# A two-layer encoder trunk: all buffers on one address residue, token sums taken from PSUM, and two projections in turns

## The chip, the cores and the metric

The kernel runs on one core of a Trainium2 chip. The metric is the device time of one execution in microseconds (us); lower is better. The core's engines are named as in the profile: PE (TensorE), DVE (VectorE), ACT (ScalarE), POOL (GpSimd) and SP (SyncE, which issues the DMAs here).

## The reference

1024 tokens of 1024 channels go through two layers in float32.

```python
for layer in range(2):
    hn = rms_norm(h, mix_norm[layer])
    mix = hybrid_mixer(hn, ...) if layer == 0 else conformer_conv(hn, ...)
    h = h + mix
    h = h + swiglu(rms_norm(h, ffn_norm[layer]), wg, wu, wd)   # (silu(h wg) * (h wu)) wd, 2816 wide
# conformer_conv: a = h w_pw1 + b; u = a[:1024] * sigmoid(a[1024:]); causal depthwise conv of
# 31 taps over the tokens; layer norm; silu; w_pw2 + b
```

`hybrid_mixer` is gated linear attention beside stick-breaking attention, then one output projection.

## The kernel before, in words

Every large product is made of three matmuls (`mm3`, L204 to L206): a float32 operand is split into a rounded part `hi` and the rest `lo`, and hi·hi, hi·lo and lo·hi are summed in PSUM. ACT writes `hi` (L89, L92), DVE writes `lo` (L90, L93); in the middle stage POOL writes the `lo` of weights. Most matmuls have 512 columns: 8708 in the program. Each reads a weight-side (stationary) and a moving operand from SBUF.

The tokens are handled in two halves of 512. The program has three stages, each with pools of its own. **Stage 1** (0 to about 880 us) holds the attention layer and `f00`, the first FFN for half 0. **Stage 2** (to about 1840 us) holds the output projection of half 1 (`out_project(1)`), the conv module (`pw1`, conv, layer norm, `pw2`) and the FFNs: `f01` (layer 0, half 1), and `f10`, the first half of layer 1's FFN weights for token half 0. **Stage 3** does the rest of layer 1's FFN by a Strassen-like scheme on pairs: sums of token blocks (`t1` to `t4`) are multiplied with sums of weight blocks (`s1` to `s4`) into PSUM tiles `ps1`, `ps2`, `ps3`.

An FFN makes `pg` and `pu` (PSUM) per chunk of 128 hidden columns, then `a` = silu(`pg`)·`pu`, split again, and `po` sums the down projection; DVE adds `po` to the residual `xr` (L228; L1159 in stage 3), which frees one of two PSUM buffers. A norm (`norm_half`) scales `x` by ACT into `xn`, PE transposes it to PSUM (`pt`, L146), and ACT and DVE split it to `hh` and `hl`.

The steps are written in the order given to `run` (L1008); a scheduler that simulates the engines then sets each engine's order, and pools of one stage reuse the addresses of the stage before, so that a first write waits for the last reader of the bytes. Weights are loaded by SP, one step ahead.

The addresses follow from the order and size of the pools. Before, in the program as built, `x` and `h` tiles start at 0 modulo 256 bytes, while `raw`, split weights `ws` and each stage's tiles (`ft`, `act`, `tt`) start at 128, because the pool `small` ahead of them ends there. Of the 8708 wide matmuls, 6848 have their two operands at different residues, and 1860 have both at 128: those in stage 2 and 3 whose `a`, `ap` or `tt` meets a weight. None has both at 0.

Of the kernel before, what the change touches and what calls it, by code (L numbers as in the profile page):

```python
# [18 lines left out]
P = 128  # L19
# [21 lines left out]
def trunk(ctx, tc, x, mix_norm, ffn_norm, hy_w_in, hy_w_gate2, hy_b_gate, hy_gla_norm,  # L41
# [194 lines left out]
    def ffn_steps(l, h, hT, xt, ps, ft, act, use_silu, group, last=NF, early=None):  # L236
# [10 lines left out]
        def chunk(f, ws):  # L247
# [20 lines left out]
            if use_silu:  # L268
                nc.scalar.activation(s, pr[0], AF.Silu)
            else:  # L270
                sigmoid(s, pr[0])
                nc.vector.tensor_mul(s, s, pr[0])  # L272
            nc.vector.tensor_mul(pr[1], s, pr[1])
            at = act(f"a{nm}")
            split(at[:, 0:TH], at[:, TH:T], pr[1])
# [82 lines left out]
    with ExitStack() as es:  # L358
# [84 lines left out]
        dec = gp.tile([P, 2, 16], F32, name="dec")  # L443
# [397 lines left out]

    with ExitStack() as es:
# [4 lines left out]
        cvp = es.enter_context(tc.tile_pool(name="cv2", bufs=8))  # L847
# [97 lines left out]
        def layer_norm(h, res):  # L945
            xn = {}

            def stats(i):
# [48 lines left out]
        def norm_step(h, gcol, name):  # L997
# [9 lines left out]
        c1 = [interleave(conv_steps(1, cs), conv_steps(1, (q,), (q,))) for cs, q in (((0, 2), 1), ((3, 5, 6, 7), 4))]  # L1007
        run([norm_step(0, mixg[1], "c0"), lambda: add_bias(0)] + p0[:2] + [norm_step(1, ffng[0], "f01")]  # L1008
            + interleave(p0[2:] + f01[:25], c0) + interleave(f01[25:31], ln0) + f01[31:]
            + [norm_step(1, mixg[1], "c1"), lambda: add_bias(1)] + p1[:4] + interleave(pw2(0, s0), c1[0])  # L1010
            + [norm_step(0, ffng[1], "f10")] + interleave(p1[4:] + f10[:9], c1[1])
            + interleave(f10[9:13], ln1) + pw2(1, s1) + [norm_step(1, ffng[1], "f11")]
            + f10[13:])
# [5 lines left out]
    with ExitStack() as es:  # L1019
# [3 lines left out]
        tp3 = es.enter_context(tc.tile_pool(name="t3", bufs=1))  # L1023
# [14 lines left out]
        (hha, hla), (hhb, hlb) = hT["f10"], hT["f11"]  # L1038
        k1, k2 = slice(0, 4), slice(4, 8)
        b11, b21, b12, b22 = [(hi[:, k, :], lo[:, k, :]) for hi, lo in ((hha, hla), (hhb, hlb)) for k in (k1, k2)]  # L1040
        t1, t3, t4 = b11, b12, b21
        tt = tp3.tile([P, NK, TH], F32R, name="tt")
        t2 = tt[:, k1, :], tt[:, k2, :]

        def whole(r, b, k):
            nc.vector.tensor_add(r, r32(b[0][:, k, :]), r32(b[1][:, k, :]))
            return r

        raw_t1 = {}

        def token_sums(k):

            r1 = raw_t1[k] = whole(s_tile(f"t1_{k}"), b11, k)
            r3 = whole(ft(f"t3_{k}"), b12, k)
            nc.vector.tensor_sub(r1, r3, r1)
            r2 = whole(ft(f"t2_{k}"), b22, k)
            nc.vector.tensor_sub(r3, r2, r3)
            nc.vector.tensor_sub(r2, r2, r1)
            for t, r in ((t2, r2), (t3, r3)):
                split(t[0][:, k, :], t[1][:, k, :], r)  # L1060

        def token_sum1(k):

            split(t1[0][:, k, :], t1[1][:, k, :], raw_t1[k])

        def token_sum4(k):

            r = whole(ft(f"t4_{k}"), b21, k)
            nc.vector.tensor_sub(r, r, r32(t2[0][:, k, :]))
            nc.vector.tensor_sub(r, r, r32(t2[1][:, k, :]))  # L1070
            split(t4[0][:, k, :], t4[1][:, k, :], r)

        def product(pm, w, b, first=True, alone=False):
            for k in range(4):
                mm3(pm, w[0][:, k, :], w[1][:, k, :], b[0][:, k, :], b[1][:, k, :], first and k == 0, k == 3,
                    skip_group_check=not alone)

        def pair_weights(w, t, f):
# [11 lines left out]
            nc.vector.tensor_sub(a2[:, k1, :], a1[:, k1, :], a2[:, k1, :])  # L1090
# [72 lines left out]
        steps, late = [lambda k=k, f=f: f(k) for f in (token_sums, token_sum1, token_sum4) for k in range(4)], []  # L1163
# [31 lines left out]
```

## Time and profile before

| | |
|---|---|
| median of 3 runs | 2355.47 us (2352.82 to 2357.84) |
| profiled execution | 2351.72 us, its span 2349.9 us |
| mean granted clock of PE | 0.988 |
| busy PE, DVE, ACT, POOL | 97%, 68%, 41%, 20% of the span |

The profile shows one execution. The span runs from its first to its last instruction. Consecutive matmuls overlap in the records, so the pace is read from start to start, not from a duration. [...]

### The profile page before, as it was taken

The numbers are of one execution on the slowest core, as the hardware profiler recorded it, in microseconds if no ns is written. First come the engines' busy times: TensorE is split into PE (matmuls) and PEld (weight loads), VectorE is DVE, ScalarE is ACT, GpSimd is POOL, SyncE is SP. The second block draws the span as 40 slices with busy tenths as digits, with TensorE's granted clock in tenths as the row PEclk, the third lists the DMA queues.
The fourth block names the chain that finished last, engine by engine and source line by source line (L and its number), as shares of the span: only waits on it lengthen the run. The fifth ranks groups of instructions, "written<-read, shape, count | busy, mean of one in ns | idle before, by whom it ended". The sixth has DMA issues, their size and how long they took to land.

```text
span 2349.9 us, 27994 instructions
## 1 busy us (share of the span) xinstructions
PE 2277.6 (97%) x10602; PEld 1856.5 (79%) x10602; DVE 1595.5 (68%) x2612; ACT 958.5 (41%) x1596; POOL 471.4 (20%) x255
## 2 busy tenths in 40 slices
PE   7999999999999999999999998999999699999999
PEld 6788878788888887888888886878877578888887
DVE  6587664877788645456666652698645877777776
ACT  6465545655565424422222244546444222222221
POOL 0000000000000004444444435949532000000000
PEclk9999999999999999999999998999999799999999
DMA  6254454233243234232232222234322133233222
GB/s 204 94 162 144 165 182 137 75 102 118 88 140 103 67 115 165 72 108 90 95 103 82 97 99 67 78 104 135 130 90 86 47 88 99 63 90 98 64 85 90
DMA packets 219637, 247.98 MB, mean 106 GB/s; under 512 B 9669, under 2 KB 169520, under 8 KB 219502
## 3 DMA queue, kind: packets, MB, share of 16 engines
q1 hardware_dynamic: 219502, 246.19, 33.1%
q8 instruction: 83, 1.36, 0.2%
q14 instruction: 52, 0.43, 0.1%
HBM read 219.42 MB, written 26.74 MB: 105 GB/s over the span
## 4 chain that ended last, share of the span: by engine, by line
PE 91%; DVE 5%; ACT 2%; issue 1%; DMA 1%; SPq 0%; DVEq 0%; ACTq 0%
PE po L204 9%; PE po L205 9%; PE po L206 9%; PE pu L204 5%; PE pu L206 4%; PE pu L205 4%; PE pg L206 4%; PE pg L204 4%; PE pg L205 4%; PE pp L204 2%; PE pp L205 2%; PE pp L206 2%; PE po L672 2%; PE wt L654 1%; PE ps3u L204 1%
## 5 line engine op out<-in xcount | busy, mean ns | idle before, releaser
L939 DVE SCALAR_TENSOR_TENSOR cs<-u,wd,cs 128x512 f32<-128x512 f32 x406 | 306.2, 754 | 10.9
L228 DVE TENSOR_TENSOR xr<-xr,po 128x512 f32<-128x512 f32 x224 | 153.1, 685 | 165.2 <-PE po L206 164.3
L90 POOL TENSOR_TENSOR wl_wo<-raw_wo,wh_wo 128x1024 fp32r<-128x1024 f32 x8 | 19.3, 2427 | 896.7 <-ACT wh_wo L89 896.7
L1159 DVE TENSOR_TENSOR xr<-xr,po 128x512 f32<-128x512 f32 x176 | 120.1, 684 | 99.1 <-PE po L206 98.8
L204 PE MATMUL po<-wh_d,a 128*128 128x512 f32 x440 | 175.5, 400 | 5.2 <-DVE xr L228 4.6
L204 PE MATMUL pg<-hh_f,wh_g 128*128 128x512 f32 x440 | 174.9, 398 | 3.6 <-DVE s L272 3.6
L206 PE MATMUL po<-wh_d,a 128*128 128x512 f32 x440 | 173.6, 395 | 2.7 <-DVE a L90 2.7
L205 PE MATMUL pg<-hl_f,wh_g 128*128 128x512 f32 x440 | 175.0, 398 | 0.0
L204 PE MATMUL pu<-hh_f,wh_u 128*128 128x512 f32 x440 | 174.7, 397 | 0.0
L206 PE MATMUL pg<-hh_f,wl_g 128*128 128x512 f32 x440 | 174.7, 397 | 0.0
L206 PE MATMUL pu<-hh_f,wl_u 128*128 128x512 f32 x440 | 174.5, 397 | 0.0
L205 PE MATMUL pu<-hl_f,wh_u 128*128 128x512 f32 x440 | 174.3, 396 | 0.0
L205 PE MATMUL po<-wl_d,a 128*128 128x512 f32 x440 | 173.7, 395 | 0.0
L89 ACT CAST wh_g<-raw_g 128x1024 fp32r<-128x1024 f32 x55 | 57.9, 1053 | 175.9 <-PE po L205 110.8
L90 POOL TENSOR_TENSOR wl_g<-raw_g,wh_g 128x1024 fp32r<-128x1024 f32 x33 | 79.5, 2409 | 136.0 <-ACT wh_g L89 136.0
L89 ACT CAST wh_d<-raw_d 128x1024 fp32r<-128x1024 f32 (+1 forms) x56 | 57.9, 1035 | 118.5 <-PE pu L205 65.6
L204 PE MATMUL pp<-hh_c,wh_p 128*128 128x512 f32 x256 | 100.6, 402 | 4.3 <-ACT hh_c L92 2.3
L204 PE MATMUL po<-wh_dp,ap 128*128 128x512 f32 x264 | 102.5, 394 | 2.3 <-DVE xr L1159 1.3
L204 PEld LDWEIGHTS po<-wh_d,a 128*128 128x128 f32 x440 | 83.3, 189 | 25.0 <-DVE xr L228 7.0
L205 PE MATMUL pp<-hl_c,wh_p 128*128 128x512 f32 x256 | 102.5, 401 | 0.0
L205 PE MATMUL po<-wl_dp,ap 128*128 128x512 f32 x264 | 101.8, 391 | 0.0
L206 PE MATMUL pp<-hh_c,wl_p 128*128 128x512 f32 x256 | 101.7, 399 | 0.0
(430 smaller groups left out, 6050.1 us busy)
## 6 DMA issues: line engine op xcount, KB each, us to landing
raw_g<-in_ffn_w_gate_dram SPq DMA_DIRECT2D x27, 1024.0 KB, 5.3
raw_u<-in_ffn_w_up_dram SPq DMA_DIRECT2D x27, 1024.0 KB, 5.4
raw_p<-in_cv_w_pw_dram SPq DMA_DIRECT2D x16, 1024.0 KB, 5.5
raw_d<-in_ffn_w_down_dram SPq DMA_DIRECT2D x14, 1024.0 KB, 5.0
raw_d<-in_ffn_w_down_dram SPq DMA_DIRECT2D x24, 512.0 KB, 3.7
raw_g<-in_ffn_w_gate_dram SPq DMA_DIRECT2D x23, 512.0 KB, 5.5
raw_u<-in_ffn_w_up_dram SPq DMA_DIRECT2D x23, 512.0 KB
raw_dp<-in_ffn_w_down_dram SPq DMA_DIRECT2D x22, 512.0 KB, 3.7
```

Source lines behind the costliest of these rows:

```text
L89: nc.scalar.copy(hi, src)
L90: (eng or nc.vector).tensor_sub(lo, src, r32(hi))
L204: nc.tensor.matmul(ps, sh, mh, start=first, stop=False, **kw)
L205: nc.tensor.matmul(ps, sh, ml, start=False, stop=False, **kw)
L206: nc.tensor.matmul(ps, sl, mh, start=False, stop=last, **kw)
L228: nc.vector.tensor_add(xt[i][:, cs], xt[i][:, cs], po)
L654: nc.tensor.transpose(pt[:, col:col + P], wrow[bi][:, P * j:P * j + P], ident)
L672: nc.tensor.matmul(po[:, lo_c:256], st["v"][j // 4][:, j % 4, e, :], m[:, 256 * jj + lo_c:256 * jj + 256], start=(last and jj == 0 and m i ...
L939: i = nc.vector.scalar_tensor_tensor(out, tap, w, acc, op0=ALU.mult, op1=ALU.add)
L1159: nc.vector.tensor_add(xres[i][:, cs], xres[i][:, cs], po)
```

## The change

Four edits stand in one diff.

1. **Addresses.** Three small tiles become one (`lv`) and `dec` is padded to 256 bytes. With this `raw`, `ws` and all stages' pools start at 0 modulo 256. In the changed program all 8708 wide matmuls have both operands at residue 0. The 128 by 128 identity stays at 128, so 652 transposes (384 before) have operands of different residues.
2. **f00.** The product of gate and up goes to the SBUF tile `s`, not back to PSUM.
3. **Token sums.** f11's norm and stage 3's `token_sums` are replaced by one step in stage 2 that makes `t1`, `t2`, `t3` and the `b22` block from the transposes in PSUM. The sign of `t3` and of its weight turns. `t2` lives in the pool `cv2`, which moves ahead of stage 2's others.
4. **pw2 in turns with pw1.** The first of the four `pw2(0)` blocks stands ahead of the second `pw1`, and the second among its first four chunks.

```diff
@@ -267,12 +267,14 @@
             s = ft(f"s{nm}")
             if use_silu:
                 nc.scalar.activation(s, pr[0], AF.Silu)
+                prod = pr[1]
             else:
                 sigmoid(s, pr[0])
                 nc.vector.tensor_mul(s, s, pr[0])
-            nc.vector.tensor_mul(pr[1], s, pr[1])
+                prod = s
+            nc.vector.tensor_mul(prod, s, pr[1])
             at = act(f"a{nm}")
-            split(at[:, 0:TH], at[:, TH:T], pr[1])
+            split(at[:, 0:TH], at[:, TH:T], prod)
             acts[f] = lambda i: (at[:, sub(i)], at[:, TH + P * (i % 4):TH + P * (i % 4) + P])
         steps, late, f = [], [], 0
@@ -440,7 +442,7 @@
         hsl = lambda h: slice(TH * h, TH * h + TH)
-        dec = gp.tile([P, 2, 16], F32, name="dec")
+        dec = gp.tile([P, 2, 32], F32, name="dec")[:, :, 0:16]
         decay = []
         def gate_weights():
@@ -839,12 +841,12 @@
+    cvp = ctx.enter_context(tc.tile_pool(name="cv2", bufs=8))
     with ExitStack() as es:
         weight_engine[0] = nc.gpsimd
         ftp = es.enter_context(tc.tile_pool(name="ft2", bufs=4))
         ap = es.enter_context(tc.tile_pool(name="act2", bufs=6))
         up = es.enter_context(tc.tile_pool(name="u2", bufs=11))
-        cvp = es.enter_context(tc.tile_pool(name="cv2", bufs=8))
         cp = es.enter_context(tc.tile_pool(name="c2", bufs=1))
         psp2 = es.enter_context(tc.tile_pool(name="ps2", bufs=1, space=PSUM))
@@ -949,9 +951,8 @@
                 if i == 0:
                     xn.update(enumerate(u_pairs(f"lx{h}")))
                 bst = small.tile([P, 2, 6], F32, name=f"bst{h}{i}", tag="bst")
-                mv = small.tile([P, 2], F32, name=f"mv{h}{i}", tag="mv")
-                rs = small.tile([P, 1], F32, name=f"lrs{h}{i}", tag="lrs")
-                nb = small.tile([P, 1], F32, name=f"lnb{h}{i}", tag="lnb")
+                lv = small.tile([P, 4], F32, name=f"lv{h}{i}", tag="lv")
+                mv, rs, nb = lv[:, 0:2], lv[:, 2:3], lv[:, 3:4]
                 pl = []
                 for j in range(2):
                     pt = ps.tile([P, 512], F32, name=f"plt{h}{i}{j}", tag="n")
@@ -1005,12 +1006,55 @@
         f10 = ffn_steps(1, 0, lambda: hT["f10"], xres, ps, ft, act, True, 4, NP, m1_d)
         c0 = conv_steps(0, range(NK))
         c1 = [interleave(conv_steps(1, cs), conv_steps(1, (q,), (q,))) for cs, q in (((0, 2), 1), ((3, 5, 6, 7), 4))]
+
+
+
+        block = lambda hi, lo, ks: ([hi[:, k, :] for k in ks], [lo[:, k, :] for k in ks])
+        blocks, raw_t1 = {}, []
+
+        def token_sums():
+            hha, hla = hT["f10"]
+            hhb, hlb = h_tile("hh_f11"), h_tile("hl_f11")
+            t2 = [[cvp.tile([P, TH], F32R, name=f"t2_{m}{k}", tag="cv") for k in range(4)] for m in range(2)]
+            for nm, hi, lo in (("1", hha, hla), ("2", hhb, hlb)):
+                blocks["1" + nm], blocks["2" + nm] = [block(hi, lo, ks) for ks in (range(4), range(4, 8))]
+            blocks["t2"] = t2
+            xt, xn, gcol = xres[4:8], u_pairs("xn_f11"), ffng[1]
+            rs = norm_stats(xt, xn, "f11")
+            for j in range(2):
+                for i in range(4):
+                    nc.scalar.mul(xn[i][j], xt[i][:, 512 * j:512 * j + 512], rs[:, i:i + 1])
+            for k in range(4):
+                pt = []
+                for kk in (k, k + 4):
+                    pt.append(ps.tile([P, 512], F32, name=f"pt_f11_{kk}", tag="n"))
+                    for i in range(4):
+                        nc.tensor.transpose(pt[-1][:, sub(i)], xn[i][kk // 4][:, sub(kk)], ident)
+                g1, g2 = gcol[:, k:k + 1], gcol[:, k + 4:k + 5]
+                r2 = cvp.tile([P, TH], F32, name=f"r2_{k}", tag="tap", bufs=2)
+                r1, r3 = u_tile(f"r1_{k}")[:, 0:TH], ft(f"r3_{k}")
+                raw_t1.append(r1)
+                nc.scalar.mul(r2, pt[1], g2)
+                b11, b12, b22 = [[m[k] for m in blocks[b]] for b in ("11", "12", "22")]
+                nc.vector.scalar_tensor_tensor(r1, pt[0], g1, r32(b11[0]), op0=ALU.mult, op1=ALU.subtract)
+                nc.vector.tensor_sub(r1, r1, r32(b11[1]))
+                nc.vector.scalar_tensor_tensor(r3, pt[0], g1, r2, op0=ALU.mult, op1=ALU.subtract)
+                split(b22[0], b22[1], pt[1], g2)
+                nc.vector.tensor_sub(r2, r2, r1)
+                split(t2[0][k], t2[1][k], r2)
+                split(b12[0], b12[1], r3)
+
+        def token_sum1():
+            for k in range(4):
+                split(blocks["11"][0][k], blocks["11"][1][k], raw_t1[k])
+
+        q0 = pw2(0, s0)
         run([norm_step(0, mixg[1], "c0"), lambda: add_bias(0)] + p0[:2] + [norm_step(1, ffng[0], "f01")]
             + interleave(p0[2:] + f01[:25], c0) + interleave(f01[25:31], ln0) + f01[31:]
-            + [norm_step(1, mixg[1], "c1"), lambda: add_bias(1)] + p1[:4] + interleave(pw2(0, s0), c1[0])
+            + [norm_step(1, mixg[1], "c1"), lambda: add_bias(1)] + q0[:1] + p1[:2]
+            + interleave(q0[1:2] + p1[2:4] + q0[2:], c1[0])
             + [norm_step(0, ffng[1], "f10")] + interleave(p1[4:] + f10[:9], c1[1])
-            + interleave(f10[9:13], ln1) + pw2(1, s1) + [norm_step(1, ffng[1], "f11")]
-            + f10[13:])
+            + interleave(f10[9:13], ln1) + pw2(1, s1) + [token_sums] + f10[13:15] + [token_sum1] + f10[15:])
@@ -1020,7 +1064,6 @@
         weight_engine[0] = nc.vector
         ap3 = es.enter_context(tc.tile_pool(name="act3", bufs=6))
         sp3 = es.enter_context(tc.tile_pool(name="s3", bufs=4))
-        tp3 = es.enter_context(tc.tile_pool(name="t3", bufs=1))
         fp3 = es.enter_context(tc.tile_pool(name="ft3", bufs=6))
         wp3 = es.enter_context(tc.tile_pool(name="w3", bufs=2))
         psp3 = es.enter_context(tc.tile_pool(name="ps3", bufs=1, space=PSUM))
@@ -1035,44 +1078,20 @@
         ft = lambda name: fp3.tile([P, 512], F32, name=name, tag="ft")
         s_tile = lambda name: sp3.tile([P, 512], F32, name=name, tag="s")
         act = lambda name: ap3.tile([P, T], F32R, name=name, tag="a")
-        (hha, hla), (hhb, hlb) = hT["f10"], hT["f11"]
         k1, k2 = slice(0, 4), slice(4, 8)
-        b11, b21, b12, b22 = [(hi[:, k, :], lo[:, k, :]) for hi, lo in ((hha, hla), (hhb, hlb)) for k in (k1, k2)]
-        t1, t3, t4 = b11, b12, b21
-        tt = tp3.tile([P, NK, TH], F32R, name="tt")
-        t2 = tt[:, k1, :], tt[:, k2, :]
-
-        def whole(r, b, k):
-            nc.vector.tensor_add(r, r32(b[0][:, k, :]), r32(b[1][:, k, :]))
-            return r
-
-        raw_t1 = {}
-
-        def token_sums(k):
-
-            r1 = raw_t1[k] = whole(s_tile(f"t1_{k}"), b11, k)
-            r3 = whole(ft(f"t3_{k}"), b12, k)
-            nc.vector.tensor_sub(r1, r3, r1)
-            r2 = whole(ft(f"t2_{k}"), b22, k)
-            nc.vector.tensor_sub(r3, r2, r3)
-            nc.vector.tensor_sub(r2, r2, r1)
-            for t, r in ((t2, r2), (t3, r3)):
-                split(t[0][:, k, :], t[1][:, k, :], r)
-
-        def token_sum1(k):
-
-            split(t1[0][:, k, :], t1[1][:, k, :], raw_t1[k])
+        t1, t2, t3, t4, b22 = [blocks[b] for b in ("11", "t2", "12", "21", "22")]
         def token_sum4(k):
-            r = whole(ft(f"t4_{k}"), b21, k)
-            nc.vector.tensor_sub(r, r, r32(t2[0][:, k, :]))
-            nc.vector.tensor_sub(r, r, r32(t2[1][:, k, :]))
-            split(t4[0][:, k, :], t4[1][:, k, :], r)
+            r = ft(f"t4_{k}")
+            nc.vector.tensor_add(r, r32(t4[0][k]), r32(t4[1][k]))
+            nc.vector.tensor_sub(r, r, r32(t2[0][k]))
+            nc.vector.tensor_sub(r, r, r32(t2[1][k]))
+            split(t4[0][k], t4[1][k], r)
         def product(pm, w, b, first=True, alone=False):
             for k in range(4):
-                mm3(pm, w[0][:, k, :], w[1][:, k, :], b[0][:, k, :], b[1][:, k, :], first and k == 0, k == 3,
+                mm3(pm, w[0][:, k, :], w[1][:, k, :], b[0][k], b[1][k], first and k == 0, k == 3,
                     skip_group_check=not alone)
         def pair_weights(w, t, f):
@@ -1087,7 +1106,7 @@
             nc.sync.dma_start(u, m1_d[t, f])
             s1 = wp3.tile([P, 4, P], F32, name=f"s1{nm}", tag="w")
             nc.vector.tensor_add(s1, a2[:, k1, :], a2[:, k2, :])
-            nc.vector.tensor_sub(a2[:, k1, :], a1[:, k1, :], a2[:, k1, :])
+            nc.vector.tensor_sub(a2[:, k1, :], a2[:, k1, :], a1[:, k1, :])
             nc.vector.tensor_sub(a1[:, k1, :], s1, a1[:, k1, :])
             nc.vector.tensor_sub(a1[:, k2, :], a1[:, k2, :], a1[:, k1, :])
             s24, s3a = parts(a1, f"s24{nm}"), parts(a2, f"s3a{nm}")
@@ -1160,7 +1179,7 @@
             return weights, body
-        steps, late = [lambda k=k, f=f: f(k) for f in (token_sums, token_sum1, token_sum4) for k in range(4)], []
+        steps, late = [lambda k=k: token_sum4(k) for k in range(4)], []
         for f in range(NP):
             mats = pair_steps(1, f)
             steps += mats[:1] + late + mats[1:]
```

The order on PE where the second `pw1` begins. `pt_c` are the transposes of its norm, `po<-wh_d` is f01's last down projection. Before:

```order
L204 MATMUL po_1_12122<-wh_d_20_110_12050,a_21_1_11881 128x512
L205 MATMUL po_1_12122<-wl_d_20_110_12051,a_21_1_11881 128x512
L206 MATMUL po_1_12122<-wh_d_20_110_12050,a_21_1_11881 128x512
L146 MATMUL pt_c_0_12175<-ident,xn_c_12130 128x128
L146 MATMUL pt_c_1_12182<-ident,xn_c_12130 128x128
L146 MATMUL pt_c_0_12175<-ident,xn_c_12132 128x128
L146 MATMUL pt_c_1_12182<-ident,xn_c_12132 128x128
L146 MATMUL pt_c_0_12175<-ident,xn_c_12134 128x128
```

Now the last rows ahead of the transposes are those of `pw2` (`wh_q`, `wl_q`):

```order
L204 MATMUL po_0_12281<-wh_q_12084,sh_11708 128x512
L205 MATMUL po_0_12281<-wl_q_12085,sh_11708 128x512
L206 MATMUL po_0_12281<-wh_q_12084,sl_11709 128x512
L204 MATMUL po_0_12281<-wh_q_12084,sh_11708 128x512
L205 MATMUL po_0_12281<-wl_q_12085,sh_11708 128x512
L206 MATMUL po_0_12281<-wh_q_12084,sl_11709 128x512
L146 MATMUL pt_c_0_12165<-ident,xn_c_12120 128x128
L146 MATMUL pt_c_1_12172<-ident,xn_c_12120 128x128
L146 MATMUL pt_c_0_12165<-ident,xn_c_12122 128x128
L146 MATMUL pt_c_1_12172<-ident,xn_c_12122 128x128
```

In all, 48 matmuls of `pw2` have come in between the last `wh_d` row and the first `pt_c` row.

The order on DVE around the last chunk of f10 (`pu_10`, then the `lo` part of `a_10`), before; `hl_f` are the splits of f11's norm, `t_..<-hh_f,hl_f` the first five of stage 3's sums:

```order
L273 TENSOR_TENSOR pu_10_0_15086<-s_10_0_15141,pu_10_0_15086 128x512
L1046 TENSOR_TENSOR t_0_15293<-hh_f_14949,hl_f_14950 128x512
L1046 TENSOR_TENSOR t_0_15296<-hh_f_14949,hl_f_14950 128x512
L1046 TENSOR_TENSOR t_1_15306<-hh_f_14949,hl_f_14950 128x512
L1046 TENSOR_TENSOR t_1_15309<-hh_f_14949,hl_f_14950 128x512
L93 SCALAR_TENSOR_TENSOR hl_f_14950<-pt_f_6_14993,vb,hh_f_14949 128x512
L1046 TENSOR_TENSOR t_2_15319<-hh_f_14949,hl_f_14950 128x512
L90 TENSOR_TENSOR a_10_0_15144<-pu_10_0_15086,a_10_0_15144 128x512
```

Now the product and the split of the same chunk stand behind the 32 operations of `token_sums` and among those of `token_sum4` (`t_0` to `t_3`):

```order
L1088 TENSOR_TENSOR t_0_15326<-t_0_15326,t_00_14892 128x512
L1088 TENSOR_TENSOR t_1_15332<-t_1_15332,t_01_14893 128x512
L1088 TENSOR_TENSOR t_2_15338<-t_2_15338,t_02_14894 128x512
L1088 TENSOR_TENSOR t_3_15344<-t_3_15344,t_03_14895 128x512
L275 TENSOR_TENSOR pu_10_0_15118<-s_10_0_15173,pu_10_0_15118 128x512
L1110 TENSOR_TENSOR raw_g_15305<-s1g_15310,raw_g_15305 128x512
L1089 TENSOR_TENSOR t_0_15326<-t_0_15326,t_10_14896 128x512
L1089 TENSOR_TENSOR t_1_15332<-t_1_15332,t_11_14897 128x512
L1089 TENSOR_TENSOR t_2_15338<-t_2_15338,t_12_14898 128x512
L1089 TENSOR_TENSOR t_3_15344<-t_3_15344,t_13_14899 128x512
L1111 TENSOR_TENSOR raw_g_15305<-raw_g_15305 128x512
L90 TENSOR_TENSOR a_10_0_15176<-pu_10_0_15118,a_10_0_15176 128x512
```

From the first token sum on, 43 rows now stand ahead of the product and 50 ahead of the split; before, the split stood behind the last row but one of the norm.

The order on DVE at the end of f00, where `oTl` are the splits for `out_project(1)`; before, among the last residual adds:

```order
L228 TENSOR_TENSOR xr_3193<-xr_3193,po_1_8274 128x512
L228 TENSOR_TENSOR xr_3195<-xr_3195,po_1_8282 128x512
L228 TENSOR_TENSOR xr_3189<-xr_3189,po_0_8296 128x512
L90 TENSOR_TENSOR oTl_8403<-ot_8552,oTh_8402 128x512
L90 TENSOR_TENSOR oTl_8403<-ot_8556,oTh_8402 128x512
L90 TENSOR_TENSOR oTl_8403<-ot_8560,oTh_8402 128x512
L228 TENSOR_TENSOR xr_3191<-xr_3191,po_0_8304 128x512
L90 TENSOR_TENSOR oTl_8403<-ot_8564,oTh_8402 128x512
```

Now they stand at f00's chunk 17 of 22, since the loads' buffers (`ft2`) no longer lie over f00's:

```order
L90 TENSOR_TENSOR oTl_8403<-ot_8408,oTh_8402 128x512
L90 TENSOR_TENSOR oTl_8403<-ot_8412,oTh_8402 128x512
L275 TENSOR_TENSOR s_17_0_7755<-s_17_0_7755,pu_17_0_7730 128x512
L90 TENSOR_TENSOR wl_u_18_0_7841<-raw_u_7834,wh_u_18_0_7840 128x1024
L228 TENSOR_TENSOR xr_3189<-xr_3189,po_0_7800 128x512
L90 TENSOR_TENSOR a_17_0_7759<-s_17_0_7755,a_17_0_7759 128x512
L90 TENSOR_TENSOR oTl_8403<-ot_8416,oTh_8402 128x512
L228 TENSOR_TENSOR xr_3191<-xr_3191,po_0_7808 128x512
L90 TENSOR_TENSOR oTl_8403<-ot_8552,oTh_8402 128x512
```

All eight splits are there in either program; now they are done some 40 DVE rows earlier.

## Rows read from the trace of the kernel before

**Rows 1.** The page, part 1: engines' busy time, share of the span, instructions.

```profile
PE 2277.6 (97%) x10602; PEld 1856.5 (79%) x10602; DVE 1595.5 (68%) x2612; ACT 958.5 (41%) x1596; POOL 471.4 (20%) x255
```

**Rows 2.** The page, part 4: the chain that ended last, by engine.

```profile
PE 91%; DVE 5%; ACT 2%; issue 1%; DMA 1%; SPq 0%; DVEq 0%; ACTq 0%
```

**Rows 3.** Timeline of PE: start, duration, then the instruction; ends of three runs.

```profile
896.23 0.40 PE L205 MATMUL po<-wl_d,a 128*128 128x512 f32 x1
...
902.74 0.39 PE L206 MATMUL po<-wh_d,a 128*128 128x512 f32 x1
...
992.80 0.40 PE L204 MATMUL pp<-hh_c,wh_p 128*128 128x512 f32 x1
...
1028.82 0.40 PE L206 MATMUL pp<-hh_c,wl_p 128*128 128x512 f32 x1
...
1406.07 0.39 PE L205 MATMUL po<-wl_d,a 128*128 128x512 f32 x1
...
1419.24 0.39 PE L206 MATMUL po<-wh_d,a 128*128 128x512 f32 x1
```

**Rows 4.** The waits of PE: total us, times, longest us.

```profile
PE ps1g L204 <- ACT tt L89: 12.6, 1, 12.6
PE pt_c L146 <- ACT xn_c L141: 7.4, 1, 7.4
PE po L204 <- DVE xr L228: 5.5, 5, 1.6
PE pp L204 <- ACT hh_c L92: 2.3, 1, 2.3
```

**Rows 5.** Windows: length, then PE, PEld, DVE, ACT, POOL busy (instructions), clock, DMA share, GB/s.

```profile
1792.27:1828.90 36.63, 30.98 (x131) 23.89 (x129) 21.75 (x32) 10.94 (x17) 7.45 (x4) 0.91 0.37 108
1828.90:1841.44 12.54, 0.00 (x0) 0.00 (x0) 12.54 (x21) 5.29 (x9) 0.00 (x0) 0.66 0.00 1
1841.44:1863.59 22.15, 15.26 (x48) 10.95 (x48) 22.15 (x37) 6.11 (x10) 0.00 (x0) 0.73 0.17 61
1792.27:1863.59 71.32, 46.24 (x179) 34.84 (x177) 56.44 (x88) 22.34 (x34) 7.45 (x4) 0.81 0.24 74
```

**Rows 6.** The same view around the norm ahead of the second pw1.

```profile
1419.30:1431.90 12.60, 2.90 (x11) 1.19 (x9) 4.54 (x16) 8.31 (x17) 4.77 (x3) 0.66 0.50 159
1431.90:1441.00 9.10, 9.10 (x36) 7.42 (x37) 2.85 (x4) 2.14 (x4) 7.09 (x4) 0.72 0.01 2
```

**Rows 7.** Timeline of DVE between f11's norm and the first products.

```profile
1790.79 1.41 DVE L93 SCALAR_TENSOR_TENSOR hl_f<-pt_f,vb,hh_f 128x512 fp32r<-128x512 f32 x2 [1.98 <-ACT hh_f L92]
...
1811.06 0.68 DVE L90 TENSOR_TENSOR a<-pu,a 128x512 fp32r<-128x512 f32 x1
...
1829.89 2.49 DVE L1046 TENSOR_TENSOR t<-hh_f,hl_f 128x512 f32<-128x512 f32 x4
```

**Rows 8.** Timeline of PE at the end of f00: the rows with idle time.

```profile
884.47 0.50 PE L204 MATMUL po<-wh_d,a 128*128 128x512 f32 x1 [0.94 <-DVE xr L228]
...
888.49 0.50 PE L204 MATMUL po<-wh_d,a 128*128 128x512 f32 x1 [0.97 <-DVE xr L228]
...
895.89 0.50 PE L204 MATMUL po<-wh_d,a 128*128 128x512 f32 x1 [1.56 <-DVE xr L228]
...
904.00 0.47 PE L204 MATMUL po<-wh_wo,oTh 128*128 128x512 f32 x1 [0.87 <-DVE xr L228]
```

**Rows 9.** Timeline of DVE in the same stretch.

```profile
892.18 3.06 DVE L90 TENSOR_TENSOR oTl<-ot,oTh 128x512 fp32r<-128x512 f32 x3
```

**Rows 10.** Timeline of POOL and DVE ahead of the second pw1.

```profile
1421.38 2.34 POOL L90 TENSOR_TENSOR wl_p<-raw_p,wh_p 128x1024 fp32r<-128x1024 f32 x1 [3.34 <-ACT wh_p L89]
...
1421.96 1.78 DVE L131 TENSOR_TENSOR s_c<-ss_c 128x4 f32<-128x4 f32 x1 [1.60 <-ACT xn_c L129]
...
1429.47 9.37 POOL L993 TENSOR_TENSOR xr<-xr,bb 128x1024 f32<-128x1024 f32 x4 [5.75 <-ACT xn_c L141]
```

**Rows 11.** Timeline of POOL in f10's last chunks.

```profile
1792.35 3.64 POOL L90 TENSOR_TENSOR wl_d<-raw_d,wh_d 128x1024 fp32r<-128x1024 f32 x2 [9.94 <-ACT wh_d L89]
```

## Prediction

> **What bounds the kernel now.** I read the engines' busy time first: PE is busy 97% of the span, DVE 68%, no other engine half of it [rows 1]. The chain that ended last is PE for 91% and DVE for 5% [rows 2]. So there are two ways to gain: a shorter pace of the matmuls themselves, and fewer of PE's waits. The timeline gives the pace [rows 3]. All three runs are unbroken streams of 512-column matmuls at the granted clock 1.00. The first, 29 starts in 6.51 us, has 232.5 ns from start to start; the second, 156 starts in 36.02 us, has 232.4; the third, 59 starts in 13.17 us, has 227.1. The list of waits then names the long ones [rows 4]: 12.6 us ahead of stage 3's first product, 7.4 and 2.3 around the norm of the second pw1, and five waits of 5.5 together on residual adds. Two stretches need windows: 1792 to 1864 [rows 5] and 1419 to 1441 [rows 6].
>
> **Addresses.** The first and the third run of [rows 3] are the same statement on tiles of the same names. In stage 1 `a`, the stationary operand, lies at residue 0 and the weights at 128; in stage 2 both lie at 128. In the second run the weights are stationary, at 128, and `hh_c` and `hl_c` move, at 0: unlike again, and slow again, whichever of the two is at 0. So what goes with the pace is whether the two lie alike modulo 256: 232.4 and 232.5 against 227.1, or 5.3 to 5.4 ns. The change makes 6848 matmuls alike that were not: 6848 x 5.3 = 36 us, 37 by the upper figure. Not all arrives: matmuls beside a wait on DVE end no earlier, and the last paces differ from run to run by some tenths. I take a seventh off: **31 us**. What no row shows is a pair with both at 0; all that are alike are at 128. Bounds from the rows: if 0 with 0 behaves like an unlike pair, the 6848 gain nothing and the 1860 now at 128 lose 5.3 ns each, +10 us; the other end is -37. I choose the end at which "alike" is what counts, since nothing in the operation names 128. Some 700 narrower matmuls become alike too and 268 transposes unlike; at 0 to 5 ns each these are -3.5 to +1.3 us, taken as nothing.
>
> [...]
>
> **Token sums.** Before, from 1792.27 to 1863.59 takes 71.3 us for 179 matmuls and transposes [rows 5]; at 0.23 us for 155 of them and 0.11 for 24 transposes this is 38 us of work. The rest is PE waiting, above all the 12.54 us in which it does nothing while DVE is busy all the time: DVE begins the last sums only at 1829.89, and takes 0.60 us for each [rows 7]. Behind it 48 matmuls take 22.15 us instead of 11, at a mean clock of 0.73.
>
> After, the sums stand ahead. They start with the first two transposed tiles, where DVE now does the first `hl` splits, at 1790.8 [rows 7]. 43 operations stand ahead of the product of chunk 10, and 50 ahead of the split of `a_10`; at 0.60 to 0.66 (PSUM source, from the two in 1.41 us) 50 x 0.63 = 31.5 us, so the split starts at 1822, where before it started at 1811.06 [rows 7]. PE waits here: the transposes of tile k+1 need the two PSUM buffers of tile k, so they go at DVE's 5 us per k, and the second halves of `pg_10` and `pu_10` stand behind the last of them. From 1795 to the split it has 24 transposes and 36 matmuls left, 11 of 27 us; the rest is a wait that takes the place of the old one. POOL makes four `wl_d` splits there, two in 3.64 us [rows 11], 7.45 us in all [rows 5]. A DVE operation with two SBUF inputs that met such a split took 1.78 us for 4 columns; it began 0.58 us after the split of 2.34 us and ended 0.02 us after it [rows 10]. So up to 7.45 us may be added, since half of the sums read SBUF twice where the `hl` splits read PSUM; I take 4. That gives 1826.
>
> [...]
>
> From 1826, 56 matmuls of the last down projection follow, 13 us at full clock and 25 at half. PE has idled by then, and the mean granted clock was 0.66 in the idle window and 0.73 in the next [rows 5], so I take half of that loss: 19 us, to 1845. Then the 48 matmuls that took 22.15 us need 11, now without a wait: 1856 against 1863.59, a gain of 8. The next products' first weight sums, which stood among the sums after 1841, no longer do: 2 more. I take **10 us**. Bounds: with no contention and the full clock 1822 + 13 + 11 = 1846, -18; with all the contention and the 104 matmuls at half clock (104 x 0.45 = 47) 1829 + 47 = 1876, +12.
>
> **pw2 in turns.** From 1419.30 to 1431.90 PE does 2.9 us of work, then 36 instructions take 9.10 us at a clock of 0.72 [rows 6]. Into this come 48 matmuls of pw2, 48 x 0.23 = 11 us, that need nothing of the norm; they are moved, not added. They cover the 7.4 and most of the 2.3 [rows 4], and PE idles no more ahead of the second window: at 1.00 instead of 0.72 its 9.10 us are 6.6, so 2.5 go, and some 0.8 more in the first. Together 13, less about 1 for the first split behind the transposes: **12 us**. The load of `raw_q` now stands ahead of `raw_p` on SP, and its two splits ahead of `wl_p` on POOL; these, 2.34 us each, were idle time before (3.34 ahead of the row at 1421.38 [rows 10]). Behind the four bias adds, 9.37 us from 1429.47, stand the `wl_p` of chunk 1, ready near 1443.6; with PE further along they are needed at about 1445. If that cover is gone each 2.4 us late comes off the 12. Bounds: -13 and -5 (two splits and their load late).
>
> **out_project(1).** The waits in [rows 8], 0.94 + 0.97 + 1.56 + 0.87 = 4.3 us, are residual adds behind `oTl` splits, as the three in a row of 3.06 us [rows 9]. The splits now come earlier, among chunks where PE has other work: **-4 us**, bounds 0 and -4.3. The edit of f00's product moves no work: 22 DVE operations write SBUF instead of PSUM, in a stage where DVE has idle time; at worst 0.1 us each on the path, 2 us. I take 0.
>
> **Sum.** 31 + 10 + 12 + 4 = 57 us. From the profiled execution's 2351.72 this gives 2294.7; the median lies 3.75 us above it, so I expect a median of **2298 us**.
>
> **Rivals.** *Addresses give nothing at 0/0.* For it: no such pair was ever seen; against it: which of the two operands is at 0 makes no difference. If residue 0 is itself slow, 2298 + 41 = 2339; else 2298 + 31 = 2329. [...] *The token sums exchange one wait for another.* For it: 50 operations ahead of `a_10`, POOL's reads beside them; against it: most of the DVE work behind 1829.89 is gone. The term is then 0: 2308. *Slower: all engines on one residue.* If what costs 5 ns is any two streams meeting on one residue, then ACT's, DVE's and PE's streams, now all at 0, meet more often. It would make every one of the 8708 matmuls dearer; it turns the whole change once it costs (10 + 12 + 4) / 8708 = 3 ns each over the old pace, and at 5 ns it gives 2355.5 - 26 + 44 = 2373. Against it: around the third run of [rows 3] ACT, DVE and POOL write `a` and weights at the residue from which PE reads, and it is the fast one. *The pw2 turn makes chunk 1 wait for `wl_p`:* 2305.
>
> **How the numbers follow.** Forecast 0.58 (its own range 2285 to 2312, which holds the pw2 rival), token sums at 0 or worse 0.17, addresses worth nothing or a loss 0.17, slower 0.04, mixtures 0.04. The range to 2330 takes in the second, half of the third and the unknown ends; downwards all good ends are 37 + 18 + 13 + 4 = 72, 2283, a little more if the narrow ones gain: 2280. A change within 0.2% (4.7 us) is about what a measurement of this kernel can't tell from none; only mixtures give that: 0.03. Slower 0.05, faster 0.92.
>
> **What would show it.** Runs of 512-column matmuls in every stage at 227 ns from start to start; one at 232 would falsify the first term. No wait of `ps1g` for `tt` in the list, and the fifth product of stage 3, again `ps3g`, some 61 us after the first `pu_10` row instead of 71.3; the waits of PE up to the split of `a_10` some 16 us together. No `pt_c` wait of 7.4, and the clock at 1.00 from 1419 to 1441. None of the waits of [rows 8]. The prediction is wrong if the pace stays, or if PE waits more than 25 us on DVE ahead of `a_10`.

## The result and the profile after

The changed kernel takes 2299.89 us in the median (4 runs, 2298.63 to 2301.31), the kernel before 2354.19 in the same comparison: a ratio of 0.9767, with a 95% interval of 0.975 to 0.9784, or 54.3 us less. The forecast was 57 us less and a median of 2298.

The page of the changed kernel, parts 1 and 4 (engines' busy time, and the chain that ended last):

```profile
PE 2242.1 (98%) x10602; PEld 1855.6 (81%) x10602; DVE 1591.4 (69%) x2600; ACT 959.5 (42%) x1596; POOL 473.9 (21%) x255
...
PE 91%; DVE 4%; ACT 2%; DMA 1%; issue 1%; POOLq 0%; SPq 0%; POOL 0%; DVEq 0%; ACTq 0%
```

PE is still what bounds, at 98% of the span and 91% of the chain: against [rows 1] its busy time fell by 35.5 us with the same number of instructions, so they come closer together. The timeline of PE, the ends of three unbroken runs, as in [rows 3]:

```profile
870.91 0.40 PE L205 MATMUL po<-wl_d,a 128*128 128x512 f32 x1
...
889.56 0.39 PE L206 MATMUL po<-wh_d,a 128*128 128x512 f32 x1
...
977.78 0.40 PE L204 MATMUL pp<-hh_c,wh_p 128*128 128x512 f32 x1
...
1012.97 0.39 PE L206 MATMUL pp<-hh_c,wl_p 128*128 128x512 f32 x1
...
1382.63 0.40 PE L205 MATMUL po<-wl_d,a 128*128 128x512 f32 x1
...
1406.67 0.39 PE L206 MATMUL po<-wh_q,sl 128*128 128x512 f32 x1
```

83 starts in 18.65 us, 156 in 35.19 and 107 in 24.04 are 227.4, 227.0 and 226.8 ns. Before, runs of the first two kinds had 232.5 and 232.4. The new pace is the one that only matmuls with both operands at 128 had, 227.1 ns in the third run of [rows 3]. Not all of stage 1 comes down quite so far: the unbroken runs of 31 to 37 matmuls in the attention layer's projections have 227.1 to 228.4 ns, where before they had 232.2 to 233.2.

The waits of PE (total us, times, longest), those that answer to [rows 4] or are new:

```profile
PE pt_f L1032 <- DVE r L1041: 5.6, 2, 3.8
...
PE po L206 <- DVE a L90: 4.1, 1, 4.1
PE pt_f L146 <- ACT xn_f L141: 3.9, 1, 3.9
...
PE po L204 <- ACT a L89: 3.6, 1, 3.6
PE po L204 <- DVE xr L228: 3.2, 1, 3.2
PE pp L204 <- ACT hh_c L92: 2.4, 1, 2.4
PE pg L204 <- ACT m L265: 1.9, 1, 1.9
...
PE ps1g L204 <- DVE xr L228: 1.3, 1, 1.3
...
PE po L204 <- ACT xn_c L129: 0.9, 1, 0.9
```

The 12.6 us of `ps1g` for `tt` and the 7.4 of `pt_c` are gone, and with them the first three waits of [rows 8]. The fourth, 0.87 us ahead of the first matmul of `out_project(1)`, is still there at 890.82; it is now put down to ACT's work for the next norm (`xn_c`). In place of those that went stand waits on the token sums (`r`), on `m`, on `a_10` (ACT, then DVE) and on the residual add behind it, 18.4 us together, 1.3 us of `ps1g`, and one of 3.9 for `xn_f` (1.2 in the trace before). The windows that answer to [rows 5] (start and end, length, then PE, PEld, DVE, ACT, POOL busy, mean clock, DMA share, GB/s) begin with the same matmul of chunk 10, and are cut at the split of `a_10`, at the first and at the fifth product of stage 3:

```profile
1755.70:1789.37 33.67, 19.14 (x76) 14.44 (x74) 32.88 (x48) 17.96 (x31) 10.95 (x4) 0.76 0.24 75
1789.37:1811.29 21.92, 16.69 (x57) 12.74 (x57) 14.01 (x22) 4.31 (x6) 0.00 (x0) 0.74 0.29 90
1811.29:1822.25 10.96, 10.96 (x48) 9.08 (x49) 6.69 (x9) 1.05 (x2) 0.00 (x0) 1.00 0.24 82
1755.70:1822.25 66.55, 46.80 (x180) 36.26 (x179) 53.57 (x77) 23.32 (x37) 10.95 (x4) 0.79 0.26 81
```

The stretch takes 66.55 us where it took 71.32 in the one execution of [rows 5]. The 48 matmuls of the first four products need 10.96 us where they needed 22.15; in exchange PE now waits ahead of them, and the mean clock is 0.76 and 0.74 there. DVE in this stretch:

```profile
1753.68 0.75 DVE L1039 SCALAR_TENSOR_TENSOR r<-pt_f,vb,hh_f 128x512 f32<-128x512 f32 x1 [1.37 <-PE pt_f L1032]
...
1783.13 2.23 DVE L1110 TENSOR_TENSOR raw_g<-s1g,raw_g 128x512 f32<-128x512 f32 x1
1785.29 3.56 DVE L1089 TENSOR_TENSOR t<-t,t 128x512 f32<-128x512 f32 x4
...
1789.37 0.68 DVE L90 TENSOR_TENSOR a<-pu,a 128x512 fp32r<-128x512 f32 x1
```

From the first sum to the split of `a_10` it is 35.7 us for 50 operations. POOL at the same time:

```profile
1778.53 7.96 POOL L90 TENSOR_TENSOR wl_d<-raw_d,wh_d 128x1024 fp32r<-128x1024 f32 x2 [19.85 <-ACT wh_d L89]
```

These two splits, 3.64 us for two such in [rows 11], took 7.96, and of the DVE operations beside them one took 2.23 where the split of `a_10` took 0.68, and four took 3.56 where four took 2.49 in [rows 7]. So both engines took longer in part of the stretch in which they ran side by side, DVE by 2.6 us here; four sums at 1780.13 took 2.48 us, no longer than those of [rows 7]. One more sum, at 1758.03, took 1.20 us, some 0.5 too many, beside the two splits before them, while two operations from PSUM ahead of it, beside the same splits, took 0.75 and 0.74 as elsewhere. The 128x4 operation of [rows 10], 1.78 us there, takes 0.16 us at 9.95 of the trace before, where POOL does nothing beside it.

Around the second pw1, two windows as long as those of [rows 6], in the same columns; the first begins with the first matmul of pw2:

```profile
1395.90:1408.50 12.60, 12.04 (x58) 9.84 (x56) 6.91 (x19) 7.31 (x15) 3.88 (x2) 1.00 0.01 2
1408.50:1417.60 9.10, 7.25 (x31) 5.80 (x32) 2.91 (x4) 5.00 (x8) 9.10 (x5) 0.81 0.00 0
```

PE works through the first window, in which it had 2.9 us of work, at a clock of 1.00. But it then waits 2.4 us for `hh_c`, and the clock of the second window is 0.81.

### The profile page after: what moved, and what is told of

It is laid out like the page before. It is cut to its first block, busy times and chain, and to the rows that moved or that the text cites. A ratio compares the mean times of both kernels' runs of the same rounds, so it can differ in the third digit from the quotient of the medians.

```text
span 2299.5 us, 28002 instructions
## 1 busy us (share of the span) xinstructions
PE 2242.1 (98%) x10602; PEld 1855.6 (81%) x10602; DVE 1591.4 (69%) x2600; ACT 959.5 (42%) x1596; POOL 473.9 (21%) x255
## 4 chain that ended last, share of the span: by engine, by line
PE 91%; DVE 4%; ACT 2%; DMA 1%; issue 1%; POOLq 0%; SPq 0%; POOL 0%; DVEq 0%; ACTq 0%
PE po L204 9%; PE po L205 9%; PE po L206 9%; PE pu L204 5%; PE pu L206 5%; PE pu L205 4%; PE pg L204 4%; PE pg L205 4%; PE pg L206 4%; PE pp L204 2%; PE pp L205 2%; PE pp L206 2%; PE po L674 2%; PE wt L656 1%; PE ps3u L204 1%
## 5 line engine op out<-in xcount | busy, mean ns | idle before, releaser
L90 POOL TENSOR_TENSOR wl_d<-raw_d,wh_d 128x1024 fp32r<-128x1024 f32 (+1 forms) x34 | 83.7, 2466 | 121.3 <-ACT wh_d L89 121.3
L204 PEld LDWEIGHTS pg<-hh_f,wh_g 128*128 128x128 f32 x440 | 83.5, 190 | 23.2 <-DVE s L273 3.8
```

Of the source, the lines that this page charges most:

```text
L90: (eng or nc.vector).tensor_sub(lo, src, r32(hi))
L204: nc.tensor.matmul(ps, sh, mh, start=first, stop=False, **kw)
```

## The experiments

Each time is a median beside the kernel before on the same chip. pad16 and pad96 are later, single executions; the time of the kernel before in their rows is that of the earlier runs on the same chip, and they have no interval. The changed kernel was not run again beside them: differences to its 2299.89 carry the 1.5 to 2.3 us by which the kernel before was faster here (2351.88 to 2352.71 against 2354.19).

| run | us | before | ratio (95%) |
|---|---|---|---|
| addr_only | 2320.66 | 2351.88 | 0.9866 (0.9851 to 0.9881) |
| pad128 | 2334.88 | 2351.88 | 0.9926 (0.9911 to 0.9941) |
| pad64 | 2335.51 | 2351.88 | 0.9930 (0.9915 to 0.9945) |
| pad32 | 2336.98 | 2351.88 | 0.9936 (0.9919 to 0.9952) |
| pw2_only | 2343.47 | 2352.71 | 0.9963 (0.9950 to 0.9977) |
| cv2_only | 2345.30 | 2352.71 | 0.9968 (0.9955 to 0.9980) |
| tok_cv2 | 2342.69 | 2352.71 | 0.9957 (0.9944 to 0.9969) |
| f00_only | 2351.47 | 2352.46 | 0.9995 (0.9986 to 1.0005) |
| chunk_first | 2292.59 | 2352.71 | 0.9744 (0.9731 to 0.9757) |
| pad16 | 2337.71 | 2352.71 | one execution |
| pad96 | 2342.83 | 2352.71 | one execution |
| chunk_first_t4 | 2285.94 | 2352.46 | 0.9718 (0.9704 to 0.9731) |

**addr_only**: the kernel before with the two edits of sizes.

```diff
-        dec = gp.tile([P, 2, 16], F32, name="dec")
+        dec = gp.tile([P, 2, 32], F32, name="dec")[:, :, 0:16]
...
-                mv = small.tile([P, 2], F32, name=f"mv{h}{i}", tag="mv")
-                rs = small.tile([P, 1], F32, name=f"lrs{h}{i}", tag="lrs")
-                nb = small.tile([P, 1], F32, name=f"lnb{h}{i}", tag="lnb")
+                lv = small.tile([P, 4], F32, name=f"lv{h}{i}", tag="lv")
+                mv, rs, nb = lv[:, 0:2], lv[:, 2:3], lv[:, 3:4]
```

> The kernel before with part 1 of the change alone (the two edits of the pools' sizes): all 8708 wide matmuls have both operands at residue 0 modulo 256, the order of the work is that of before. Theory 'alike modulo 256': every unbroken run of 512-column matmuls has a pace of about 227 ns, and the time falls by 28 to 34 us, from 2354 to about 2323. Rival 'the addresses are worth nothing, the other three parts made the 54 us': 2354, within 5. Rival 'residue 0 is slow as such': 2360 to 2365.

Measured: 31.2 us less. Its timeline of PE, the same two statements as in the last two runs of [rows 3]:

```profile
983.85 0.40 PE L204 MATMUL pp<-hh_c,wh_p 128*128 128x512 f32 x1
...
1019.03 0.39 PE L206 MATMUL pp<-hh_c,wl_p 128*128 128x512 f32 x1
...
1388.81 0.39 PE L205 MATMUL po<-wl_d,a 128*128 128x512 f32 x1
...
1401.98 0.39 PE L206 MATMUL po<-wh_d,a 128*128 128x512 f32 x1
```

The first went from 232.4 to 227.0 ns, the second stayed at 227.1. In the two traces all 10602 PE instructions stand in the same order, so the addresses alone do it; both rivals fall.

**pad128, pad64, pad32, pad16, pad96**: the changed kernel with a pad ahead of the weights' pools (here 128 bytes; 16, 8, 4 and 24 words in the others), which moves the weights and all stages' tiles against `x` and `h`.

```diff
+    pad_p = ctx.enter_context(tc.tile_pool(name="pad", bufs=1))
+    nc.vector.memset(pad_p.tile([P, 32], F32, name="pad"), 0.0)
     weights_es = ctx.enter_context(ExitStack())
```

> The changed kernel with 128 bytes of pad ahead of the weights' pools, so that 6848 matmuls have unlike operands again (0 and 128) and 1860 both at 128; everything else as changed. Theory 'alike modulo 256': the pace of the unlike goes back to 232 ns, and the time rises by 28 to 34 us, from 2300 to about 2331. Rival 'the addresses are worth nothing': 2300, within 5.

> The changed kernel with 64 bytes of pad at the same place: 6848 matmuls have one operand at 0 and one at 64, 1860 both at 64. Theory 'alike modulo 256' (any difference of residue costs 5 ns): 2331, as with 128. Rival 'only the half of 256 bytes counts, that is whether the operands differ by an odd multiple of 128': 2300. Rival 'any start off a 256-byte line costs, also where both are alike': 2331 + 8.

> The changed kernel with 32 bytes of pad at the same place: one operand at 0 and one at 32, or both at 32. Theory 'alike modulo 256': 2331. Rival 'a difference below 64 bytes costs nothing': 2300.

> The changed kernel with 16 bytes of pad ahead of the weights' pools. Theory 'any difference modulo 256 costs': both kinds of products at 232 to 234 ns, about 2335 us. Rival 'below 32 bytes nothing is lost': 227 ns and 2300.

> The changed kernel with 96 bytes of pad at the same place. With 64 bytes the products with the moving operand at 64 and the stationary at 0 ran at 228.8 ns, those the other way round at 233.3; with 32 and 128 both ways cost 232 to 233. Theory 'the price hangs on the offset between the two streams, and 64 the one way is an exception': both at 232 to 234 ns, about 2336 us. Rival 'the moving operand may stand 64 bytes or more behind': the products with it at 96 run at 229.

Measured: 2334.9, 2335.5, 2337.0, 2337.7 and 2342.8, so some 35 to 43 us above the changed kernel for every offset. From unbroken runs like those above, in ns, the down projection of f00 (weights move, `a` at 0 is stationary) and pw1 (`hh_c` at 0 moves, weights are stationary):

| weights at | weights move | weights stationary |
|---|---|---|
| 0 (changed kernel) | 227.4 | 227.0 |
| 16 | 233.4 | 233.4 |
| 32 | 233.2 | 233.4 |
| 64 | 228.9 | 233.3 |
| 96 | 233.3 | 234.2 |
| 128 | 232.3 | 232.4 |

The rows of two of these, pad64 first; with the pad's two lines each line number is two higher:

```profile
881.14 0.39 PE L207 MATMUL po<-wl_d,a 128*128 128x512 f32 x1
...
899.91 0.40 PE L208 MATMUL po<-wh_d,a 128*128 128x512 f32 x1
...
989.55 0.39 PE L206 MATMUL pp<-hh_c,wh_p 128*128 128x512 f32 x1
...
1025.71 0.39 PE L208 MATMUL pp<-hh_c,wl_p 128*128 128x512 f32 x1
```

Here 83 starts in 18.77 us and 156 in 36.16.

```profile
884.04 0.40 PE L207 MATMUL po<-wl_d,a 128*128 128x512 f32 x1
...
903.17 0.40 PE L208 MATMUL po<-wh_d,a 128*128 128x512 f32 x1
...
993.61 0.39 PE L206 MATMUL pp<-hh_c,wh_p 128*128 128x512 f32 x1
...
1029.91 0.39 PE L208 MATMUL pp<-hh_c,wl_p 128*128 128x512 f32 x1
```

Here 83 in 19.13 and 156 in 36.30. "Alike modulo 256" holds for the time: 16 bytes cost as much as 128 (2337.7 us against 2334.9). Two details were not forecast. With 64 bytes the one way round costs only 1.5 ns, so neither that theory nor a rival is exact there. And 96 bytes cost the most, 43 us by one execution. The rival by which pairs alike at 64 would cost too, 8 us more, falls with the total of 2335.5, and with the pace of such a pair, f01's down projection in pad64:

```profile
1396.46 0.39 PE L208 MATMUL po<-wh_d,a 128*128 128x512 f32 x1
...
1416.22 0.39 PE L208 MATMUL po<-wh_d,a 128*128 128x512 f32 x1
```

These are 88 starts in 19.76 us, or 227.1 ns with both operands at 64. So in these runs it is not the weights' own address that costs, but its offset from the other operand's.

**pw2_only**: the kernel before with the new order of pw2.

```diff
+        q0 = pw2(0, s0)
...
-            + [norm_step(1, mixg[1], "c1"), lambda: add_bias(1)] + p1[:4] + interleave(pw2(0, s0), c1[0])
+            + [norm_step(1, mixg[1], "c1"), lambda: add_bias(1)] + q0[:1] + p1[:2]
+            + interleave(q0[1:2] + p1[2:4] + q0[2:], c1[0])
```

> The kernel before with part 4 alone: the blocks of pw2 in turns with pw1; addresses as before. Theory: the wait of 7.4 us ahead of the transposes of the norm c1 and most of the half clock behind it go, and are not given back: 2354 - 12 = 2342. Rival 'given back later': the trace of the changed kernel shows 3.9 us of waiting for xn_f at the next norm where before there were 1.2, and 2.4 us for hh_c are still there: 2354 - 8 = 2346. Rival 'hidden anyway': 2354.

Measured: 9.2 us less, and in the list of its waits:

```profile
PE pt_f L146 <- ACT xn_f L141: 3.2, 1, 3.2
...
PE pp L204 <- ACT hh_c L92: 2.2, 1, 2.2
```

The 7.4 us of `pt_c` are gone; `hh_c` still waits 2.2 us, and the next norm 3.2 where it had waited 1.2. So it is the first rival: some 2 us are given back later, and some 2 are never gained.

**cv2_only**: the kernel before with the pool first in its stage, which moves `ft2` off f00's tiles.

```diff
         weight_engine[0] = nc.gpsimd
+        cvp = es.enter_context(tc.tile_pool(name="cv2", bufs=8))
         ftp = es.enter_context(tc.tile_pool(name="ft2", bufs=4))
...
-        cvp = es.enter_context(tc.tile_pool(name="cv2", bufs=8))
```

> The kernel before with the pool cv2 as the first of stage 2's pools (still inside the stage) and nothing else, so that ft2 no longer lies over f00's tiles. Theory: the four waits on residual adds at the end of f00 go from 5.0 us to 1: 2354 - 4 = 2350. Rival 'the order of the splits does not matter to the time': 2354.

Measured: 7.4 us less (4.7 to 10.6 by the interval), more than expected. Its waits:

```profile
PE ps1g L204 <- ACT tt L89: 15.6, 1, 15.6
...
PE po L204 <- DVE xr L228: 3.5, 4, 1.4
```

The residual adds wait 2 us less in all than in [rows 4], with one of 1.4 us that is new near 1800. At the end of f00, from the first matmul of the last chunk's `pu` to the first of `out_project(1)`, it takes 28.70 us (869.39 to 898.09) where it took 32.10 (871.90 to 904.00), 3.4 us less. The waits there are one of 0.66 us and the fourth of [rows 8], 0.87, which stays. The rest lies in the stretch of [rows 5]: from chunk 10's matmul to the fifth product of stage 3 it takes 67.48 us, although `ps1g` now waits 15.6 for `tt`. The scheduler gave DVE another order there:

```profile
1798.96 0.69 DVE L90 TENSOR_TENSOR a<-pu,a 128x512 fp32r<-128x512 f32 x1 [0.65 <-ACT a L89]
...
1816.73 5.50 DVE L1046 TENSOR_TENSOR t<-hh_f,hl_f 128x512 f32<-128x512 f32 x9
```

The split of `a_10` now starts 13.0 us after that matmul, ahead of all sums; before it started 18.8 us after it, behind the first five. The waits on `a_10` are gone. Why the scheduler chose so was not tried.

**tok_cv2**: the kernel before with part 3 alone: `token_sums`, `token_sum1`, the new `token_sum4`, the sign of `t3` and the pool `cv2` as in the change, without the parts 1, 2 and 4.

```diff
-            + interleave(f10[9:13], ln1) + pw2(1, s1) + [norm_step(1, ffng[1], "f11")]
-            + f10[13:])
+            + interleave(f10[9:13], ln1) + pw2(1, s1) + [token_sums] + f10[13:15] + [token_sum1] + f10[15:])
```

> The kernel before with part 3 alone (the token sums from PSUM, with the pool cv2 ahead of stage 2): addresses, pw2 and the product of f00 as before. Theory as in the prediction: 10 us for the sums and 4 for the move of the pool, 2340. Rival 'one wait for another': the trace of the changed kernel has 66.5 us from chunk 10's first half to the fifth product where before there were 71.3, at a shorter pace of the matmuls; then the sums give 4 and the pool 4, 2346. Rival 'the sums give nothing': 2350.

Measured: 10.0 us less (7.3 to 13.2 by the interval). Beyond the pool alone that is 2.6, which the two intervals can't tell from nothing. Its waits:

```profile
PE pt_f L1031 <- DVE r L1040: 5.6, 2, 3.8
PE po L204 <- DVE xr L228: 5.0, 3, 3.5
...
PE po L204 <- ACT a L89: 4.1, 1, 4.1
...
PE po L206 <- DVE a L90: 3.5, 1, 3.5
```

They are those of the changed kernel, within 0.6 us but for the residual adds' total. The stretch of [rows 5] in pw2_only, which leaves it as it was, in cv2_only and here:

```profile
1784.09:1854.16 70.07, 44.24 (x180) 32.97 (x178) 56.41 (x88) 22.27 (x34) 7.48 (x4) 0.84 0.25 75
...
1785.96:1853.44 67.48, 43.09 (x180) 33.18 (x178) 55.44 (x88) 22.30 (x34) 7.30 (x4) 0.83 0.27 78
...
1790.36:1857.31 66.95, 46.99 (x180) 36.24 (x179) 53.60 (x77) 23.61 (x37) 11.54 (x4) 0.80 0.27 81
```

So one execution of an unchanged stretch can differ from the 71.32 of [rows 5] by more than 1 us (f00_only has 70.11), and sums and pool together shorten it by 3.1 to 4.4 us, where 10 were forecast for the sums. The order that cv2_only happened to get gives 2.6 to 3.8 there without the sums. The end of f00 takes 28.72 us, as in cv2_only. The time lies between the first rival's 2346 and the theory's 2340, but for the sums the rival's 4 us is the better figure.

**f00_only**: the kernel before with the product in `s`.

```diff
+                prod = pr[1]
             else:
                 sigmoid(s, pr[0])
                 nc.vector.tensor_mul(s, s, pr[0])
-            nc.vector.tensor_mul(pr[1], s, pr[1])
+                prod = s
+            nc.vector.tensor_mul(prod, s, pr[1])
...
-            split(at[:, 0:TH], at[:, TH:T], pr[1])
+            split(at[:, 0:TH], at[:, TH:T], prod)
```

> The kernel before with part 2 alone: f00's product goes to the SBUF tile. Theory as in the prediction: nothing, 2352.5 within 3. Rival: the parts tried alone sum to 50.4 us (31.2, 9.2, 10.0), the whole change gives 52 to 54, and the rest of 2 to 4 is this edit: 2349 to 2350.

Measured: 1.0 us less, with 0 in the interval: no difference that can be told, although the scheduler gave PE another order within f00.

**chunk_first**: the changed kernel with chunk 10 ahead of the sums.

```diff
-            ... + [token_sums] + f10[13:15] + [token_sum1] + f10[15:])
+            ... + f10[13:15] + [token_sums, token_sum1] + f10[15:])
```

> The changed kernel with the last two steps of f10 (the down projection before it and chunk 10) ahead of the token sums in the list of steps; then 8 operations instead of 43 stand on DVE between the first sum and the product of chunk 10. Theory 'what the sums cost is that chunk 10 and its down projection wait behind them': the waits of 3.6, 4.1 and 3.2 us on a_10 and on the residual add and the half clock around them go; 72 matmuls lie over the sums, and the time falls by 6 to 12 us from 2300, to about 2291. Rival 'DVE sets the end of this stretch': some 68 operations in a row stand ahead of the first product's weights whatever the order, and the wait moves to ps1g: 2298 to 2302.

Measured: 2292.59, 7.3 us below the changed kernel. Its waits:

```profile
PE ps1g L204 <- ACT wh_s24g L89: 13.6, 1, 13.6
...
PE po L204 <- DVE xr L228: 1.5, 2, 1.2
```

The waits on `a_10` are gone, and one of 13.6 us for the first product's weights has come: their parts stand on DVE behind and among the sums. Both were right in part: the price of the sums is what waits behind them on DVE, and then DVE's row of work sets the end.

**chunk_first_t4**: chunk_first, with `t4` made only ahead of the product that reads it.

```diff
+            while waiting:
+                token_sum4(waiting.pop(0))
             product(p2, a22, t4, first=False)
...
-        steps, late = [lambda k=k: token_sum4(k) for k in range(4)], []
+        waiting, steps, late = list(range(4)), [], []
```

> The changed kernel with chunk 10 and the down projection ahead of the token sums (as in the run before), and with the four sums for t4 made only ahead of the one product that reads them. With chunk 10 ahead, PE waited 13.7 us in one piece for the first product's weights, whose parts stood on DVE among the 16 operations for t4. Theory 'DVE's row of work ahead of the first product sets the end': 16 operations of 0.60 us come out of it, 9.7 us less of waiting, and the time falls from 2292.6 to about 2284. Rival 'the wait moves to the product that reads t4, or to the loads': 2289 to 2293.

Measured: 2285.94, 6.7 us less again, 14.0 below the changed kernel and 66.5 below the one before. Its waits:

```profile
PE ps1g L204 <- ACT wh_s24g L89: 6.4, 1, 6.4
...
PE po L204 <- DVE xr L228: 1.5, 2, 1.2
```

The wait fell by 7.2 of the 9.7 us expected, and none above 0.6 us took its place. This is the fastest version.

## Why the prediction was right, point by point

**The total came out nearer than its terms, and that is in part luck.** The forecast was 31 + 10 + 12 + 4 + 0 = 57. Tried alone the parts give 31.2, 10.0 for sums and pool together, 9.2 for pw2 and 1.0 for f00's product: 51.4, against 54.3 for all. So 57 was 5.6 too much for the parts, above all in the sums with the pool (14 forecast) and in pw2 (12), and half of that came back because the whole gave 2.9 more than its parts. With intervals of some 3 us on each part, that 2.9 can't be told from noise.

**Addresses: right in cause and size.** The gap of the prediction, no pair at 0 and 0 in any row, is closed: 227 ns. The cut of a seventh fits the kernel before (31.2), though waits are not its only reason: the matmuls of the attention layer's runs gain 4.1 to 5.3 ns, most of them less than the 5.3 of the sum. With the other parts in place the same offset is worth 35 to 37 us (pad128 against the changed kernel, by their times or by their distances from the kernel before), but the interval of addr_only, 28 to 35 us, reaches to 35, so it is not shown that more of it arrives there.

**Token sums: right in direction, 10 us was too much.** The split of `a_10` came 33.7 us after the first matmul of the stretch, where 1826 - 1792.27 = 33.7 was forecast, with about 3 us more on DVE beside POOL's splits (2.6 and 0.5) as against 4, an estimate from the one operation of 1.78 us. PE's waits up to it are 15.2 us (16 forecast). The step that failed is the one behind: "19 us, to 1845" for the 56 matmuls, and "2 more". From the split to the first product it took 21.9, with two waits of 3.2 and 1.3 on residual adds that the sum did not have. The 2 us of the next products' weight sums were counted twice, since 48 matmuls in 11 us have no wait left to lose. So the stretch takes 66.55, not 61, and the gain there is 3.5 to 4.8 us, according to which execution of the old stretch it is held against (70.07 or 71.32). It is nearly the second rival, one wait for another: PE waits 18.4 us on the sums and what stands behind them. The half clock of the forecast stands in the trace of the kernel before: from 1836 to 1846.5 the clock is 0.50, and 11 matmuls start there from 1842.04 to 1846.30, or 0.43 us apart, where the bound had 0.45.

**pw2 in turns: mechanism right, 9.2 instead of 12.** The wait of 7.4 went. The step that failed is "most of the 2.3" and "PE idles no more": the split behind the transposes still waits 2.4 us, the clock of the window behind it is 0.81 and not 1.00, and the norm after that waits longer. `wl_p` of chunk 1 was no trouble.

**out_project(1): right at its place, but the pool does more.** The first three waits of [rows 8] went, 3.47 us together, and the end of f00 is 3.4 us shorter in cv2_only and in tok_cv2. The fourth, 0.87, was not behind the `oTl` splits alone, as the sum had it, since it stays without them. The further 3 us or so of cv2_only lie in the stretch of [rows 5], where the sum had put down nothing for the pool.

## What to carry to other kernels

Where PE bounds, read its pace from start to start in long unbroken runs, and compare runs that differ in nothing but their tiles' addresses: 1.3 to 1.5% of this kernel's time lay in 128 bytes ahead of a pool. Work that is pulled forward to fill a wait pushes back all that stands behind it on its engine; let the last producer that another engine waits for go ahead of it, as chunk 10 did here (6 to 7 us). And a total that comes out right does not show that its terms are: the parts run alone, and the traces of their stretches, did.

## What was not expected of the hardware

In these runs the pace of 512-column matmuls goes with the offset between the moving and the stationary operand in SBUF modulo 256 bytes, in steps that are not a simple function of it: 226.8 to 228.4 ns at 0, 232 at 128, 233.4 at 16, 234.2 at 96 with the weights stationary, and 228.9 against 233.3 at 64 depending on which of the two moves. What in the chip makes it so was not tried.
